# Interleaved RoPE on one core: row 0 loaded whole in fp32 and cast by ScalarE

## The chip, the cores and the metric

The kernel runs on one core of one Trainium2 chip. The metric is device microseconds (us) of one execution; of several timed runs the median is taken. Lower is better.

## What is computed

`x` has the shape (8, 2048, 16, 64) in fp32: 8 batch entries of 2048 positions, 16 heads of 64 elements. Each neighbouring pair of elements is rotated by an angle that depends on the position:

```python
x1, x2 = x[..., 0::2], x[..., 1::2]      # pairs
out1 = x1 * cos - x2 * sin               # cos, sin: (2048, 32), broadcast over batch and heads
out2 = x1 * sin + x2 * cos
out  = interleave(out1, out2)            # same shape as x, fp32
```

In and out are 67.1 MB each, so some 134 MB of fp32 have to cross between HBM and the on-chip memory (SBUF).

## The kernel before

**Tiling.** A "row" here is one batch entry. Its 2048 positions are spread over the 128 partitions, 16 positions to each (K = 16), so a row holds 16 x 1024 = 16384 elements in each partition: 64 KB in fp32, 32 KB in bf16. There are 8 rows, 0 to 7.

**Buffers.** `rows_sb` has five slots (NX = 5) of one row each in bf16. `slot(b)` sends rows 0, 1, 2 to slots 2, 3, 4 and rows 3 to 7 to slots 0 to 4. So rows 5, 6 and 7 reuse the slots of rows 0, 1 and 2, and slots 0 and 1 are empty until rows 3 and 4 are loaded into them. The buffer with the tag "work" is shared by `head` (four positions of row 0 in fp32), by `qt` (the scratch product of a rotation) and by `tail`.

**Loads and stores.** `load` and `store` issue DMAs from the POOL queue. A load casts fp32 to bf16 on the way in, and a store casts bf16 to fp32 on the way out. One DMA may move two or three rows. The exceptions are the first 4 of the 16 positions of row 0 (HEAD = 4), which come in fp32 over the SP queue into `head` and are cast by ScalarE (ACT), and the last 4 positions of row 7 (TAIL = 4), which are cast to fp32 by ScalarE and leave over the SP queue.

**Rotation.** `rotate(b, k0, k1)` is three VectorE (DVE) operations on positions k0 to k1 of a row: the product with the signed sine table into `qt` (line 83), the product with the cosine table in place (line 84), and the sum of the row with the pair-swapped `qt` (line 91). The two tables are built in bf16 from the loaded `sin` and `cos` by three small DVE operations (lines 104 to 106).

**Order.** The order is written out by hand (`manual_schedule`), and every engine and every queue works its own list from front to back. On POOL: the rest of row 0 (line 58), `cos`, `sin` (lines 97 and 98), rows 1+2 and rows 3+4 (line 60), then the stores of rows 0+1 (line 67) and 2 (line 65), the loads of row 5 and of rows 6+7 into the slots that these stores free, and the stores of rows 3 to 5, 6 and 7. On DVE: tables, row 0 in two parts (4 and 12 positions), row 1, row 2 in two halves, rows 3 to 7. A one-element copy `mark` on ScalarE, in the middle of the first half of row 2, and another one on row 0 (lines 114 and 115) hold the store of rows 0+1 back until DVE is that far. Near the end a one-element copy on ScalarE into row 6's slot (line 133) holds the last cast back until the store of row 6 has left.

Of the kernel before, what the change touches and what calls it, by code (L numbers as in the profile page):

```python
# [2 lines left out]

# [4 lines left out]


@with_exitstack  # L10
def kernel(
    ctx: ExitStack,
    tc: tile.TileContext,
    x: bass.AP,
    cos: bass.AP,
    sin: bass.AP,
    out: bass.AP,
):
    nc = tc.nc
    fp32 = mybir.dt.float32  # L20
    bf16 = mybir.dt.bfloat16
    mult = mybir.AluOpType.mult
    add = mybir.AluOpType.add

    B, S, H, D = x.shape
    P = 128
    K = S // P
    D2 = D // 2
    HD = H * D
    NX = 5  # L30
    HEAD = 4
    TAIL = 4
    HALF = 8

    x_t = x.rearrange("b (p k) h d -> p b k (h d)", p=P, k=K)
    out_t = out.rearrange("b (p k) h d -> p b k (h d)", p=P, k=K)
    cos_t = cos.rearrange("(p k) c -> p (k c)", p=P, k=K)
    sin_t = sin.rearrange("(p k) c -> p (k c)", p=P, k=K)

    consts = ctx.enter_context(tc.tile_pool(name="consts", bufs=1))  # L40
    stage = ctx.enter_context(tc.tile_pool(name="stage", bufs=1))

    cos_sb = consts.tile([P, K * D2], fp32)
    sin_sb = consts.tile([P, K * D2], fp32)
    c_tab = consts.tile([P, K, D], bf16)
    s_tab = consts.tile([P, K, D], bf16)
    mark = consts.tile([1, 1], bf16)


    def slot(b):  # L50
        return b - 3 if b >= 3 else b + 2

    rows_sb = consts.tile([P, NX, K, HD], bf16)

    def load(b, n=1, k0=0):
        s = slot(b)
        if n == 1:
            nc.gpsimd.dma_start(out=rows_sb[:, s, k0:], in_=x_t[:, b, k0:])  # L58
        else:
            nc.gpsimd.dma_start(out=rows_sb[:, s : s + n], in_=x_t[:, b : b + n])  # L60

    def store(b, n=1, k1=K):
        s = slot(b)
        if n == 1:
            nc.gpsimd.dma_start(out=out_t[:, b, :k1], in_=rows_sb[:, s, :k1])  # L65
        else:
            nc.gpsimd.dma_start(out=out_t[:, b : b + n], in_=rows_sb[:, s : s + n])  # L67

    def rotate(b, k0=0, k1=K, between=None):

        nk = k1 - k0
        xp = rows_sb[:, slot(b), k0:k1]
        qt = stage.tile([P, K, HD], bf16, name="qt", tag="work")

        def rows(a):
            return a.rearrange("p k (h e) -> p k h e", h=H, e=D)

        def tab(a):
            return dataclasses.replace(
                a, offset=a.offset + k0 * D, ap=[a.ap[0], [D, nk], [0, H], [1, D]]  # L80
            )

        nc.vector.tensor_tensor(out=rows(qt[:, :nk]), in0=rows(xp), in1=tab(s_tab), op=mult)  # L83
        nc.vector.tensor_tensor(out=rows(xp), in0=rows(xp), in1=tab(c_tab), op=mult)  # L84
        if between is not None:
            between()
        q_swap = dataclasses.replace(
            qt, offset=qt.offset + 1, ap=[qt.ap[0], [2, nk * HD // 2], [-1, 2]]
        )
        x3 = xp.rearrange("p k (a j) -> p (k a) j", j=2)  # L90
        nc.vector.tensor_tensor(out=x3, in0=x3, in1=q_swap, op=add)  # L91

    with tc.manual_schedule():
        head = stage.tile([P, HEAD, HD], fp32, name="st", tag="work")
        nc.sync.dma_start(out=head, in_=x_t[:, 0, :HEAD])
        load(0, k0=HEAD)
        nc.gpsimd.dma_start(out=cos_sb, in_=cos_t)  # L97
        nc.gpsimd.dma_start(out=sin_sb, in_=sin_t)  # L98
        load(1, 2)
        load(3, 2)  # L100

        nc.scalar.copy(out=rows_sb[:, slot(0), :HEAD], in_=head)  # L102
        s2 = s_tab.rearrange("p k (i j) -> p (k i) j", j=2)
        nc.vector.tensor_copy(out=s2[:, :, 0], in_=sin_sb)  # L104
        nc.vector.tensor_scalar_mul(s2[:, :, 1], sin_sb, -1.0)  # L105
        nc.vector.tensor_copy(  # L106
            out=c_tab.rearrange("p k (i j) -> p (k i) j", j=2),
            in_=cos_sb.to_broadcast([P, K * D2, 2]),
        )
        rotate(0, 0, HEAD)  # L110
        rotate(0, HEAD, K)
        rotate(1)

        rotate(2, 0, HALF, lambda: nc.scalar.copy(out=mark, in_=rows_sb[:1, slot(2), 0, :1]))  # L114
        nc.scalar.copy(out=rows_sb[:1, slot(0), 0, :1], in_=rows_sb[:1, slot(0), 0, :1])  # L115
        store(0, 2)
        rotate(2, HALF, K)
        store(2)
        load(5)
        load(6, 2)  # L120
        rotate(3)
        rotate(4)
        rotate(5)
        store(3, 3)
        rotate(6)
        store(6)
        rotate(7)
        store(7, k1=K - TAIL)


        tail = stage.tile([P, TAIL, HD], fp32, name="st", tag="work")
        last = rows_sb[:, slot(7)]
        nc.scalar.copy(out=rows_sb[:1, slot(6), 0, :1], in_=last[:1, K - 1, :1])  # L133
        nc.scalar.copy(out=tail, in_=last[:, K - TAIL :])  # L134
        nc.sync.dma_start(out=out_t[:, B - 1, K - TAIL :], in_=tail)


# [1 line left out]
_INS = ['x', 'cos', 'sin']  # L139
_OUTS = [((8, 2048, 16, 64), 'float32')]  # L140


# [23 lines left out]
```

## Time and profile before

| what | value |
|---|---|
| median of 3 runs | 316.18 us (316.08 to 316.18) |
| the profiled execution, its time | 316.1 us |
| the profiled execution, its span in the trace | 314.3 us |
| VectorE busy | 210.8 us, 67% of the span |
| ScalarE busy | 8.9 us, 3% |
| HBM read and written | 67.63 MB and 67.11 MB, 429 GB/s over the span |
| queue q0 (POOL), share of the 16 DMA engines | 96.8% |
| queue q1 (SP), share of the 16 DMA engines | 3.3% |

The span is what the trace covers; the profiled execution's time is 1.8 us longer. A DMA is worked by 16 DMA engines that each serve 8 of the 128 partitions. The GB/s of a stretch count the bytes as they are on the SBUF side of a load and on the HBM side of a store. A load that casts fp32 to bf16 therefore shows half of what it reads, and a store shows what it writes.

### The profile page before, as it was taken

To read this page: it belongs to the slowest core of one execution; us is meant where nothing else is said; L and a number is where in the kernel's file an instruction comes from. 1 tells how busy PE (TensorE), PEld (TensorE's weight loads), DVE (VectorE), ACT (ScalarE), POOL (GpSimd) and SP (SyncE) were. 2 spreads that over 40 slices of the span, in tenths; PEclk is the share of its full clock that TensorE was granted. 3 is DMA by queue.
4 is the path that set the end of the run, shared out by engine and by line. 5 is a ranking of instruction groups with operands and counts; after the bars stand their busy time and mean duration, and the time that the engine had idled before them with its cause. 6 is when DMAs were issued, how large, how long until landed. Compare 5 with 4: busy or idle time off the path is not lost.

```text
span 314.3 us, 116 instructions
## 1 busy us (share of the span) xinstructions
DVE 210.8 (67%) x33; ACT 8.9 (3%) x6; POOL 7.8 (2%) x16
## 2 busy tenths in 40 slices
DVE  0009995099999999999993399903999999200000
ACT  1040000000000000000000000000000000000400
POOL 4000000000000000000000000000000000000000
DMA  8999999999999999999999999999999999999997
GB/s 256 261 284 200 200 204 263 200 200 217 250 200 267 442 492 400 400 475 459 400 200 246 221 200 200 250 217 334 400 509 425 400 400 525 409 400 400 434 434 334
DMA packets 2656, 102.24 MB, mean 325 GB/s; under 512 B 224, under 2 KB 224, under 8 KB 352
## 3 DMA queue, kind: packets, MB, share of 16 engines
q0 software_dynamic: 2368, 98.04, 96.8%
q1 hardware_dynamic: 288, 4.19, 3.3%
HBM read 67.63 MB, written 67.11 MB: 429 GB/s over the span
## 4 chain that ended last, share of the span: by engine, by line
another core or an unknown queue 66%; DVE 20%; ACTq 1%; ACT 0%; issue 0%; DVEq 0%
DVE rows_sb L84 7%; DVE qt L83 7%; DVE rows_sb L91 6%; ACTq L161 1%; DVE c_tab L106 0%; ACT rows_sb L133 0%; ACT mark L114 0%; ACT rows_sb L115 0%; ACTq L133 0%; DVEq L83 0%
## 5 line engine op out<-in xcount | busy, mean ns | idle before, releaser
L83 DVE TENSOR_TENSOR qt<-rows_sb,s_tab 128x16384 bf16<-128x16384 bf16 (+3 forms) x10 | 69.8, 6984 | 33.7 <-DMA rows_sb<-in_x_dram 33.5
L91 DVE TENSOR_TENSOR rows_sb<-rows_sb,qt 128x16384 bf16<-128x16384 bf16 (+3 forms) x10 | 69.8, 6985 | 0.6 <-ACT mark L114 0.3
L84 DVE TENSOR_TENSOR rows_sb<-rows_sb,c_tab 128x16384 bf16<-128x16384 bf16 (+3 forms) x10 | 69.8, 6984 | 0.3
L104 DVE CAST s_tab<-sin_sb 128x512 bf16<-128x512 f32 x1 | 0.5, 454 | 23.8 <-DMA sin_sb<-in_sin_dram 23.8
L133 ACT COPY rows_sb<-rows_sb 1x1 bf16<-1x1 bf16 x1 | 0.2, 193 | 196.5 <-DMA out_dram<-rows_sb 196.5
L67 POOL DMA_DIRECT2D out_dram<-rows_sb x2 | 1.5, 740 | 138.5 <-ACT rows_sb L115 93.7
L102 ACT CAST rows_sb<-st 128x4096 bf16<-128x4096 f32 x1 | 3.6, 3604 | 13.2 <-DMA st<-in_x_dram 13.2
L65 POOL DMA_DIRECT2D out_dram<-rows_sb x3 | 1.7, 567 | 80.4 <-DVE rows_sb L91 80.4
L134 ACT CAST st<-rows_sb 128x4096 f32<-128x4096 bf16 x1 | 3.6, 3598 | 0.0
L60 POOL DMA_DIRECT2D rows_sb<-in_x_dram x3 | 2.2, 740 | 18.8 <-DMA out_dram<-rows_sb 18.8
L114 ACT COPY mark<-rows_sb 1x1 bf16<-1x1 bf16 x1 | 0.2, 193 | 78.7 <-DVE rows_sb L84 78.7
L58 POOL DMA_DIRECT2D rows_sb<-in_x_dram x2 | 1.2, 609 | 24.3 <-DMA out_dram<-rows_sb 23.5
L102 ACT ACT_TABLE_LOAD x1 | 1.3, 1283 | 0.7 <-PEq L150 0.7
L106 DVE CAST c_tab<-cos_sb 128x1024 bf16<-128x1024 f32 x1 | 0.7, 685 | 0.0
L98 POOL DMA_DIRECT2D sin_sb<-in_sin_dram x1 | 0.6, 564 | 0.0
L97 POOL DMA_DIRECT2D cos_sb<-in_cos_dram x1 | 0.6, 557 | 0.0
L105 DVE TENSOR_SCALAR s_tab<-sin_sb 128x512 bf16<-128x512 f32 x1 | 0.4, 444 | 0.0
L115 ACT COPY rows_sb<-rows_sb 1x1 bf16<-1x1 bf16 x1 | 0.2, 189 | 0.0
L150 POOL MEMSET const-float32-0.0<- 128x1 f32 x1 | 0.1, 99 | 0.2 <-issue 0.2
L150 POOL MEMSET const-bfloat16-1.0<- 128x1 bf16 x1 | 0.1, 102 | 0.0
L150 POOL MEMSET const-float32-1.0<- 128x1 f32 x1 | 0.1, 99 | 0.0
L150 POOL MEMSET const-uint8-127<- 128x1 uint8 x1 | 0.1, 99 | 0.0
## 6 DMA issues: line engine op xcount, KB each, us to landing
rows_sb<-in_x_dram POOLq DMA_DIRECT2D x3, 8192.0 KB, 59.4
out_dram<-rows_sb POOLq DMA_DIRECT2D x1, 6144.0 KB, 40.9
rows_sb<-in_x_dram POOLq DMA_DIRECT2D x1, 4096.0 KB, 38.3
rows_sb<-in_x_dram POOLq DMA_DIRECT2D x1, 3072.0 KB, 21.2
st<-in_x_dram SPq DMA_DIRECT2D x1, 2048.0 KB, 14.5
out_dram<-st SPq DMA_DIRECT2D x1, 2048.0 KB, 15.5
cos_sb<-in_cos_dram POOLq DMA_DIRECT2D x1, 256.0 KB, 21.2
sin_sb<-in_sin_dram POOLq DMA_DIRECT2D x1, 256.0 KB, 21.3
```

The lines of the kernel that those rows point to most:

```text
L58: nc.gpsimd.dma_start(out=rows_sb[:, s, k0:], in_=x_t[:, b, k0:])
L60: nc.gpsimd.dma_start(out=rows_sb[:, s : s + n], in_=x_t[:, b : b + n])
L65: nc.gpsimd.dma_start(out=out_t[:, b, :k1], in_=rows_sb[:, s, :k1])
L67: nc.gpsimd.dma_start(out=out_t[:, b : b + n], in_=rows_sb[:, s : s + n])
L83: nc.vector.tensor_tensor(out=rows(qt[:, :nk]), in0=rows(xp), in1=tab(s_tab), op=mult)
L84: nc.vector.tensor_tensor(out=rows(xp), in0=rows(xp), in1=tab(c_tab), op=mult)
L91: nc.vector.tensor_tensor(out=x3, in0=x3, in1=q_swap, op=add)
L97: nc.gpsimd.dma_start(out=cos_sb, in_=cos_t)
L102: nc.scalar.copy(out=rows_sb[:, slot(0), :HEAD], in_=head)
L106: nc.vector.tensor_copy(out=c_tab.rearrange("p k (i j) -> p (k i) j", j=2), in_=cos_sb.to_broadcast([P, K * D2, 2]),)
L134: nc.scalar.copy(out=tail, in_=last[:, K - TAIL :])
L161: with _tile.TileContext(nc) as tc:
```

## The change

Row 0 no longer comes in two pieces. One DMA of the SP queue brings all of it in fp32 into `wide`, a view of slots 0 and 1 (2 x 32 KB in each partition, 64 KB in fp32). ScalarE casts it in four parts of four positions each into slot 2. The load of rows 3+4, which goes to slots 0 and 1, is written behind these casts. VectorE rotates row 0 in four parts of four positions, where it took two parts before. The POOL queue's first load (the 12 positions of row 0) and the buffer `head` are gone.

```diff
-    HEAD = 4
+    PART = 4
...
+    wide = rows_sb[:, :2].rearrange("p s k e -> p (s k e)").bitcast(fp32)
+    wide = wide.rearrange("p (k e) -> p k e", k=K)
+
-    def load(b, n=1, k0=0):
+    def load(b, n=1):
         s = slot(b)
         if n == 1:
-            nc.gpsimd.dma_start(out=rows_sb[:, s, k0:], in_=x_t[:, b, k0:])
+            nc.gpsimd.dma_start(out=rows_sb[:, s], in_=x_t[:, b])
...
-        head = stage.tile([P, HEAD, HD], fp32, name="st", tag="work")
-        nc.sync.dma_start(out=head, in_=x_t[:, 0, :HEAD])
-        load(0, k0=HEAD)
+
+        nc.sync.dma_start(out=wide, in_=x_t[:, 0])
         nc.gpsimd.dma_start(out=cos_sb, in_=cos_t)
         nc.gpsimd.dma_start(out=sin_sb, in_=sin_t)
         load(1, 2)
+
+        for k in range(0, K, PART):
+            nc.scalar.copy(out=rows_sb[:, slot(0), k : k + PART], in_=wide[:, k : k + PART])
         load(3, 2)
-
-        nc.scalar.copy(out=rows_sb[:, slot(0), :HEAD], in_=head)
         s2 = s_tab.rearrange("p k (i j) -> p (k i) j", j=2)
...
-        rotate(0, 0, HEAD)
-        rotate(0, HEAD, K)
+        for k in range(0, K, PART):
+            rotate(0, k, k + PART)
         rotate(1)
```

## The prediction

> **What bounds the kernel now.** I read the page's head and its DMA rows first, then the windows around the start, the first store and the end, and then the timeline of VectorE and POOL up to that store.
>
> ```profile
> DMA  8999999999999999999999999999999999999997
> ...
> q0 software_dynamic: 2368, 98.04, 96.8%
> q1 hardware_dynamic: 288, 4.19, 3.3%
> HBM read 67.63 MB, written 67.11 MB: 429 GB/s over the span
> ```
>
> The DMA engines are full in every slice but the first and the last, while VectorE works 67% of the span. The windows show how little is left:
>
> ```profile
> 0.00:2.00 2.00, 0.00 (x0) 1.26 (x1) 0.96 (x6) 1.00 0.45 98
> 62.00:98.00 36.00, 35.15 (x6) 0.29 (x2) 0.00 (x0) 1.00 1.00 215
> 98.00:100.00 2.00, 2.00 (x1) 0.00 (x0) 0.71 (x1) 1.00 0.46 98
> 100.00:102.00 2.00, 2.00 (x1) 0.00 (x0) 0.00 (x0) 1.00 1.23 524
> 312.00:314.30 2.30, 0.00 (x0) 0.00 (x0) 0.00 (x0) 1.00 0.27 114
> ```
>
> The last two columns are the DMA share and GB/s. Packets are counted where they start, so short windows swing (0.46, then 1.23: one round falls into the next window); a long one shows the pace, 215 GB/s of bf16, which is 430 of fp32 read. The first packet starts at 2.0 us and the last ends near 313.4 (packet records of the trace), so 134.74 MB take 311.4 us: 433 GB/s, 27.0 for each of 16 engines. A row of 8.39 MB is 19.4 us; one partition's 64 KB, of which every engine has 8 in a row, is 2.42 us. So 311 of 314.3 us are bytes at this pace. A change that moves the same bytes can only pay by the rest, or cost by opening a hole. A hole opens where a transfer is issued too late. The places near the change:
>
> ```profile
> 15.27 3.60 ACT L102 CAST rows_sb<-st 128x4096 bf16<-128x4096 f32 x1 [13.25 <-DMA st<-in_x_dram]
> 23.80 0.45 DVE L104 CAST s_tab<-sin_sb 128x512 bf16<-128x512 f32 x1 [23.80 <-DMA sin_sb<-in_sin_dram]
> ...
> 25.08 2.29 DVE L83 TENSOR_TENSOR qt<-rows_sb,s_tab 128x4096 bf16<-128x4096 bf16 x1
> 27.40 2.29 DVE L84 TENSOR_TENSOR rows_sb<-rows_sb,c_tab 128x4096 bf16<-128x4096 bf16 x1
> 29.73 2.29 DVE L91 TENSOR_TENSOR rows_sb<-rows_sb,qt 128x4096 bf16<-128x4096 bf16 x1
> ...
> 62.46 8.69 DVE L83 TENSOR_TENSOR qt<-rows_sb,s_tab 128x16384 bf16<-128x16384 bf16 x1 [10.67 <-DMA rows_sb<-in_x_dram]
> ...
> 98.14 0.71 POOL L67 DMA_DIRECT2D out_dram<-rows_sb  x1 [93.69 <-ACT rows_sb L115]
> ```
>
> VectorE is done with row 0 at 51.8 and waits 10.67 us for rows 1+2, which land at 62.4. From there runs the one tight chain: row 1 (26.2 us), half of row 2 and the two marks, the store of rows 0+1 at 98.14. Its first packets start at 100.4, right behind the last load: a lead of 2.3 us, part of which the issue itself needs. Whatever delays VectorE's start on row 1 eats this lead and then leaves the engines idle.
>
> **The change part by part.**
>
> *Bytes.* Row 0 is 8.39 MB of fp32 read whichever queue brings it. Both queues go at one pace: between 3 and 5 us the SP queue alone moves 426 to 475 GB/s; the casting loads read 430. A casting load writes half as much into SBUF, and the trace shows no gain in pace from that. The sum until rows 1+2 are in is the same 25.7 MB (row 0, tables 0.52, two rows): 59.4 us from 2.0 on, and the landing stays near 62.4. 0 us.
>
> *Start.* SP issues at 0.74 us as before. The POOL queue, first issued at 1.24, has its first packets at 5.6; until then SP's queue feeds the engines alone, before with 8 packets of 16 KB for each engine (4.9 us of work), now with 8 of 64 KB (19.4 us). Covered in both, 0 us. The first round of packets is slower than the later ones (mean 1.12 us where 0.61 follows): half a microsecond of latency. As a fixed latency it stays; as a factor on the packet it would grow (third rival).
>
> *Row 0's landing.* Head and POOL queue took turns packet by packet: 5 of 8 head packets were through at 5.6, the other 3 each waited for a turn of 48 KB read (2.42 us for the pair), which gives 12.9, one more turn before the completion 14.7, and it landed at 15.24. Now each turn of SP is 2.42 us, and what POOL's queue has first is small: the tables, 8 packets of 4 KB an engine at 0.16 us and two completions. With 2 of SP's 8 packets through at 5.6 us the other 6 alternate with 6 of these. Row 0 is through after 2.4 + 8 x 2.42 + 6 x 0.16 = 22.7 us and, with skew and completion as above, lands at about 23.5; the tables land at about 24 (23.8 before). Rows 1+2 then have the engines to themselves.
>
> The Trainium skill (DMA: Bandwidth & Descriptors, Queues, rings and completion order) says that an engine drains a whole packet, typically 9 to 17 descriptors, from one ring before it turns to the next. By that all of row 0 would pass in one turn and land about 1 us earlier. The trace differs: the head, 8 such pieces an engine, would then have landed near 7 us, and it landed at 15.24.
>
> *Casts.* Four of 3.60 us (line 102, the same shape) in place of one: 23.5 to 37.9. Behind them on ScalarE stand only the marks, due at 97.5.
>
> *Rotation of row 0.* Four parts of 25.08 to 32.05 = 6.97 us, 27.9 in place of 26.7. The first waits for the first cast, at 27.1; the later ones find theirs done (3.6 beside 7.0 us). VectorE is done at 55.1 in place of 51.8. Cover: it would wait for 62.4 anyway, so 7.3 us are left of the 10.67. 0 us.
>
> *The load of rows 3+4.* Its issue moves from 3.7 to 37.9, since POOL stands in its queue until the last cast. Queued behind it on POOL is the store of rows 0+1, due at 98. The engines need this load at 62.4, when rows 1+2 run out. Cover 24.5 us; even with the longest time seen from an issue to first packets (1.24 to 5.6, 4.4 us) 20 us remain. 0 us. If the cover were gone, each us of lateness would cost one us.
>
> *After 62.4.* Waits, order and sizes are those of before. One DMA less on POOL saves its completion, 0.02 us of each engine.
>
> Sum: 0 us on 316.1 of the profiled execution; the median of the runs shown is 0.08 above it. I forecast 316.15.
>
> **The rivals.**
>
> *SP's row 0 is cut into small packets and starves (slower).* No transfer of q1 with over 16 KB in a partition is in the trace: 288 packets are 256 of 16 KB and 32 completions. If the queue cuts at 16 KB, row 0 has 32 packets an engine, 5 of them gone at 5.6 us. Ten go with the tables until 13, and the rest alternate one for one with 16 packets of 2.42 us of rows 1+2, the last of which are through only near 62. Then row 0 lands at 62: casts to 76.5; load of rows 3+4 issued there; VectorE's parts 65.7 to 93.6, row 1 to 119.8, the rest of the chain (9.5 us) to 129.3. The store comes 31.2 us late, less the lead 2.3: +28.9, 345 us. It decides where row 0 lands after about 31 us (62.4 less 27.9 and the first cast); cut at 32 KB (16 packets) it lands at 30 to 32, which costs 0 to 1. Against: every large packet seen is one partition's whole run: 16 KB on q1, 64 KB in q0's stores (2048 data packets carry 97.5 MB). 0.06.
>
> The Trainium skill (DMA: Bandwidth & Descriptors, SWDGE vs HWDGE vs iDMA) puts a packet of the software queue at preferably 4096 bytes or less. If the SP queue held to that, row 0 would starve as in this rival; the trace's tables do so (128 packets of 4 KB for 512 KB), its rows do not.
>
> *Parts don't overlap (the change doesn't do what it says).* If VectorE's first part waited for all four casts, it would run 37.9 to 65.8, 3.4 us past 62.4, less the lead: +1.1, 317.2. Against: in the order of the compiled instructions each part has its own wait on ScalarE. 0.02.
>
> *The slow first round is a factor.* 1.12 against 0.61 on a 2.42 us packet is 2.0 us lost where 0.5 is lost now: +1.5, 317.6. For it: nothing but the bound. 0.05.
>
> *Faster.* Idle are the first 2.0 us, 0.2 around 3 us and the end; the change touches only the 0.2. Beyond 0.63 us I see no source but one the trace doesn't show. 315.3, 0.04.
>
> **How the numbers follow.** 0.2% is 0.63 us, about what a measurement of this kernel can tell from no change. The forecast, in which all of it stays covered, has 0.83 and by itself spans 315.8 to 316.5 (the runs' 0.1 us, the start's 0.2, another 0.2 in landings). Reaching to the small slower costs (lead partly used up, a 32 KB cut, part of the first-round bound) the range is 315.7 to 317.1. The starving case is left out at the top. Faster 0.04, same 0.83, slower 0.13.
>
> **What would show it.** Right: casts start near 23.5 and end near 38; POOL's issue of rows 3+4 near 38; VectorE still waits some 7 us for a DMA at 62.4; the store of rows 0+1 at 98.1; no slice of the DMA row under 9 but the ends. Wrong: casts that start after 31 us, a first row-1 product later than 62.5, or a hole in the DMA row between 62 and 105.

## The result, and the profile after

The changed kernel takes 316.80 us, median of 22 runs (316.56 to 317.42), against 316.15 for the kernel before. The ratio is 1.0015 (95% interval 1.0009 to 1.0021): slower by some 0.5 us by the ratio and by 0.65 us by the medians, which is small, but clear of no change. The time lies inside the range, and the ratio inside the 0.2% that I called "same", though its interval just reaches past it; the forecast of no change at all was wrong.

The page of the changed kernel, with the same rows as before: its slices, its queues, its HBM bytes.

```profile
DMA  9999999999999999999999999999999999999997
...
q0 software_dynamic: 2224, 94.90, 92.1%
q1 hardware_dynamic: 288, 10.49, 8.0%
HBM read 67.63 MB, written 67.11 MB: 428 GB/s over the span
```

Row 0 has moved from q0 to q1. q1 still has 288 packets, with 6.3 MB more in them: in the packet records 128 packets of 64 KB bring row 0, where 128 of 16 KB brought its head, so SP's queue did not cut it. HBM bytes are the same and the DMA row has no hole. The windows (the last two columns are the DMA share and GB/s):

```profile
0.00:2.00 2.00, 0.00 (x0) 1.27 (x1) 0.94 (x6) 1.00 1.29 426
62.00:98.00 36.00, 35.03 (x6) 0.29 (x2) 0.00 (x0) 1.00 0.98 211
98.00:100.00 2.00, 2.00 (x1) 0.00 (x0) 0.70 (x1) 1.00 0.92 197
100.00:102.00 2.00, 2.00 (x1) 0.00 (x0) 0.00 (x0) 1.00 1.23 524
312.00:314.50 2.50, 0.00 (x0) 0.00 (x0) 0.00 (x0) 1.00 0.26 111
```

The load of rows 3+4 hands over to the store of rows 0+1 between 98 and 102 as it did before; that the first window has 426 means only that the first packets are larger and are counted whole where they start. The timeline of the steps that the prediction named:

```profile
23.56 14.13 ACT L104 CAST rows_sb<-rows_sb 128x4096 bf16<-128x4096 f32 x4 [21.55 <-DMA rows_sb<-in_x_dram]
23.88 0.46 DVE L107 CAST s_tab<-sin_sb 128x512 bf16<-128x512 f32 x1 [23.88 <-DMA sin_sb<-in_sin_dram]
...
27.20 2.29 DVE L86 TENSOR_TENSOR qt<-rows_sb,s_tab 128x4096 bf16<-128x4096 bf16 x1 [1.96 <-ACT rows_sb L104]
...
37.98 0.73 POOL L63 DMA_DIRECT2D rows_sb<-in_x_dram  x1 [34.78 <-ACT rows_sb L104]
...
62.58 8.69 DVE L86 TENSOR_TENSOR qt<-rows_sb,s_tab 128x16384 bf16<-128x16384 bf16 x1 [7.30 <-DMA rows_sb<-in_x_dram]
...
98.26 0.70 POOL L70 DMA_DIRECT2D out_dram<-rows_sb  x1 [59.55 <-ACT rows_sb L118]
```

Row 0 lands at 23.56, the casts end at 37.7, POOL issues at 37.98, VectorE waits another 7.30 us for rows 1+2, and everything from there on is 0.12 us later than before. Inside the kernel the picture is the predicted one, but for one sign: the first product of row 1, at 62.58, is past the 62.5 that the prediction set as a mark of being wrong. The kernel before with a later load of rows 3+4 (the first of the two below) has 62.58 too and takes the time of before, so that mark was set inside the scatter.

Where, then, is the difference? Each run has a time and a span, and most of the difference lies outside what the trace covers:

| | time, us | span, us | time outside the span, us |
|---|---|---|---|
| before, profiled execution | 316.1 | 314.3 | 1.8 |
| after, profiled execution | 316.64 | 314.5 | 2.1 |
| before, median of 33 runs beside the first experiments | 316.17 | 314.4 | 1.77 (1.73 to 1.83) |
| after, median of 22 runs | 316.80 | 314.65 | 2.15 (2.12 to 2.20) |

The larger part, 0.38 us, is outside the span, and the two ranges do not touch. Some 0.2 us are inside it.

### The profile page after: what moved, and what is told of

The parts are those of the page before. It is cut to its first block, busy times and chain, and to the rows that moved or that the text cites. A ratio compares the mean times of both kernels' runs of the same rounds, so it can differ in the third digit from the quotient of the medians.

```text
span 314.5 us, 126 instructions
## 1 busy us (share of the span) xinstructions
DVE 211.9 (67%) x39; ACT 19.4 (6%) x9; POOL 7.3 (2%) x15
## 4 chain that ended last, share of the span: by engine, by line
another core or an unknown queue 51%; DMA 20%; DVE 20%; ACT 1%; ACTq 1%; issue 0%; DVEq 0%
DMA out_dram<-rows_sb 13%; DMA rows_sb<-in_x_dram 7%; DVE rows_sb L87 7%; DVE qt L86 7%; DVE rows_sb L94 6%; ACT rows_sb L104 1%; ACTq L164 1%; ACT rows_sb L136 0%; ACT mark L117 0%; ACT rows_sb L118 0%; DVEq L86 0%; ACTq L136 0%
## 5 line engine op out<-in xcount | busy, mean ns | idle before, releaser
L86 DVE TENSOR_TENSOR qt<-rows_sb,s_tab 128x16384 bf16<-128x16384 bf16 (+2 forms) x12 | 70.2, 5847 | 32.6 <-DMA rows_sb<-in_x_dram 30.2
L94 DVE TENSOR_TENSOR rows_sb<-rows_sb,qt 128x16384 bf16<-128x16384 bf16 (+2 forms) x12 | 70.2, 5847 | 0.6 <-ACT mark L117 0.3
L87 DVE TENSOR_TENSOR rows_sb<-rows_sb,c_tab 128x16384 bf16<-128x16384 bf16 (+2 forms) x12 | 70.2, 5847 | 0.4
L104 ACT CAST rows_sb<-rows_sb 128x4096 bf16<-128x4096 f32 x4 | 14.1, 3602 | 21.5 <-DMA rows_sb<-in_x_dram 21.5
L63 POOL DMA_DIRECT2D rows_sb<-in_x_dram x3 | 2.2, 722 | 53.5 <-ACT rows_sb L104 34.8
L61 POOL DMA_DIRECT2D rows_sb<-in_x_dram x1 | 0.5, 546 | 23.5 <-DMA out_dram<-rows_sb 23.5
```

The lines of the kernel that those rows point to most:

```text
L104: nc.scalar.copy(out=rows_sb[:, slot(0), k : k + PART], in_=wide[:, k : k + PART])
```

## The experiments

Below, "outside" is the median over a kernel's runs of time less span. "Records" are all of VectorE's entries in the trace, its waits and synchronisation included: 47 before, 55 after (six products and two semaphore waits more). Every kernel stands beside runs of the kernel before on the same chip.

### The time outside the span: VectorE's list

**Six more products alone** (kernel before, row 0 in four parts):

```diff
-        rotate(0, HEAD, K)
+        for k in range(HEAD, K, HEAD):
+            rotate(0, k, k + HEAD)
```

> Kernel before with one edit: VectorE rotates the 12 positions of row 0 in three parts of four, so that it issues the 6 more products of the change and nothing else moves. Instruction theory (the change's 0.35 us outside the span comes from VectorE's longer list): time outside the span 2.1 us where before has 1.8, span 314.3, in all +0.3 to +0.4 us. Rival (the cost comes with row 0's new path over SP): outside 1.8, +0.0.

Measured: 316.16 beside 316.17, outside 1.76, 53 records. The instruction theory failed as stated.

**The six products taken out of the changed kernel:**

```diff
-        for k in range(0, K, PART):
-            rotate(0, k, k + PART)
+        rotate(0, 0, PART)
+        rotate(0, PART, K)
```

> Changed kernel with VectorE's two parts of row 0 (4 and 12 positions) as before: 6 products fewer than the changed kernel, the transfer and the four casts kept. VectorE then waits for the last cast at 37.7 and is done at 57.5, before rows 1+2 land at 62.5. Instruction theory: outside 1.8, in all 0.3 to 0.4 us below the changed kernel, so +0.1 to +0.2 against before. Rival: outside stays 2.1, time that of the changed kernel, +0.5 to +0.6.

Measured: 316.36, outside 1.77, span 314.6, 47 records. Here the instruction theory held: the 0.38 us are gone, though SP's load, the casts and the late load are all in place. So it does hang on VectorE's list, and yet six more instructions do not bring it by themselves. Either it needs ScalarE's three more casts too (a limit on the whole program), or VectorE's list has a limit between 53 and 55 records.

**Nine more products** (kernel before), and **14 ScalarE copies** (kernel before):

```diff
-        rotate(0, HEAD, K)
+        for k in range(HEAD, K, 3):
+            rotate(0, k, k + 3)
```

> Kernel before with the 12 positions of row 0 in four parts of three: 9 more products on VectorE (56 records of it in the trace, 55 in the changed kernel, 53 in the run with 6 more), nothing on ScalarE. If VectorE's own list passes a limit between 53 and 55 records: outside 2.15, +0.4 us. If the limit lies in the whole program or needs ScalarE's three more casts: outside 1.77, +0.0.

```diff
         nc.scalar.copy(out=rows_sb[:, slot(0), :HEAD], in_=head)
+        for _ in range(14):
+            nc.scalar.copy(out=mark, in_=head[:1, 0, :1])
```

> Kernel before with 14 one-element ScalarE copies behind the head's cast, at a time when ScalarE idles: 130 records in the whole trace or more, where the changed kernel has 126, VectorE's list as before. If the limit is one on the whole program: outside 2.15, +0.4 us. If it is VectorE's own: outside 1.77, +0.0.

Measured: with nine more products 316.56 (ratio 1.0010, 1.0002 to 1.0019), outside 2.19, span 314.4 as before; with the copies 316.14, outside 1.77, at 130 records in the whole trace. It is VectorE's list, not the program's length.

**Three products fewer** (kernel before, `rotate(0)` in one part):

> Kernel before with row 0 rotated in one part: 3 products fewer on VectorE, done with row 0 at 51.5 as before. If the time outside the span goes by steps, this either stays on the step of before (1.77, 0.0) or reaches a lower one (1.4, -0.4 us, a version faster than both); if it went by the instruction, 0.06 us for each (0.38 over 6): outside 1.6, -0.2.

Measured: 316.15, outside 1.76, 44 records. No lower step, and nothing by the instruction.

I then took it for a limit: 54 or 55 records and more cost 0.4 us. The changed kernel with four SP loads (below) spoilt this: 57 records, outside 1.81. Three kernels told a limit from a window:

```diff
+        nc.vector.tensor_copy(out=mark, in_=sin_sb[:1, :1])
         rotate(0, 0, HEAD)
-        rotate(0, HEAD, K)
+        for k in range(HEAD, K, 3):
+            rotate(0, k, k + 3)
```

> Kernel before with row 0 in five parts and one more one-element VectorE copy: 57 VectorE records (56 gave 2.19 us outside the span; the changed kernel with four SP loads has 57 and gave 1.81). Window theory (VectorE's list costs 0.4 us where its end falls in a narrow range of lengths): outside 1.8. Limit theory (every list from 54 or 55 on costs it, and the four SP loads took it away in some other way): outside 2.15.

The same copy in front of four parts of four:

> Kernel before with row 0 in four parts and one more one-element VectorE copy: 54 VectorE records, between 53 (1.76) and 55 (2.15). It places the lower edge; both theories allow either value: 1.77 or 2.15, nothing in between.

And seven parts (4 and six of 2), without it:

> Kernel before with the 12 positions of row 0 in six parts of two: 15 more products, some 62 VectorE records. VectorE is done with row 0 near 53, covered. Window theory: outside 1.8. Limit theory: outside 2.15 or more.

Measured: outside 1.75 with 57 records, 2.04 with 54, and 1.81 with 62. One VectorE instruction more than the five parts makes the kernel faster: 316.24 where those have 316.56 (in another set, whose kernel before has 316.17 where this one's has 316.13). At 54 records neither theory's "nothing in between" holds: 2.04 (2.02 to 2.08) is lower than 2.15.

If that is so, the changed kernel must get faster by instructions that do nothing for it. One-element copies behind its tables (line 113 on), first two, then three of them:

```diff
+        for _ in range(3):
+            nc.vector.tensor_copy(out=mark, in_=sin_sb[:1, :1])
         for k in range(0, K, PART):
             rotate(0, k, k + PART)
```

> Changed kernel with two one-element VectorE copies added behind the tables: 57 VectorE records, past the window of 54 to 56. Window theory: outside 1.77, so 0.38 us faster than the changed kernel for more instructions. The rest of the loss, if it is the first round of 64 KB packets, stays: span 0.2 above before, 316.35 in all.

> Changed kernel with three one-element VectorE copies behind the tables (two gave 56 VectorE records, still in the window): 57 records. Window theory: outside 1.77, 0.38 us below the changed kernel. First-round theory: span 0.2 above before, as in the other runs with 64 KB packets, 316.35 in all.

Two copies made 56 records, not the 57 that I had counted on, and stayed inside the window: 316.97, outside 2.17. Three made 57: 316.40, outside 1.75 (1.72 to 1.81), where the changed kernel beside the first of these two has 316.72 and 2.16:

> The changed kernel itself beside these two, on one chip: 316.7 to 316.8, outside 2.15, span 0.2 above before. All theories give the same here; it is the base for the two others.

All that was measured of it, by length of VectorE's list:

| records | kernel | outside, us |
|---|---|---|
| 44 | before, row 0 in one part | 1.76 |
| 47 | before; changed with two parts; before with 14 ScalarE copies | 1.77; 1.77; 1.77 |
| 47 | before with rows 3+4 held back, less and more (below) | 1.80; 1.81 |
| 48 | changed, SP in two loads and two parts; before, head in two loads (both below) | 1.77; 1.75 |
| 53 | before, four parts | 1.76 |
| 54 | before, four parts, one copy | 2.04 |
| 55 | changed | 2.15 and 2.16 |
| 56 | before, five parts; changed, two copies; changed, SP in two loads | 2.19; 2.17; 2.17 |
| 57 | before, five parts, one copy; changed, three copies; changed, SP in two loads, one copy | 1.75; 1.75; 1.77 |
| 57 | changed, SP in four loads | 1.81 |
| 62 | before, seven parts | 1.81 |

The window is shown, on both kernels. What happens in it is not. The Trainium skill (Runtime: NRT & Kernel Launch, Instruction fetch mechanics) says that an engine's instructions are fetched in blocks ahead of their use and that crossing a block's end costs little, mostly hidden. A block's end that falls among the last instructions of VectorE, where no work hides its fetch, would give such a window. This is a guess, and the kept traces do not bear it out. Their packet records hold a queue for instructions, q14: in every kernel its packets of 8 KB start 7.3 to 10.6 us ahead of the span. A single one lies behind a span, 1.2 us after the end of the kernel with seven parts (62 records), which does not have the 0.4 us. Behind the spans of the kernels with 54, 55 and 56 records there is none, as far as the trace reaches. What else shifts with the length of the list is open.

### The 0.2 us inside the span: the first packets

**SP's load in two pieces** (changed kernel), so that the first 8 packets of each engine are of 16 KB again:

```diff
-        nc.sync.dma_start(out=wide, in_=x_t[:, 0])
+        nc.sync.dma_start(out=wide[:, :PART], in_=x_t[:, 0, :PART])
+        nc.sync.dma_start(out=wide[:, PART:], in_=x_t[:, 0, PART:])
```

> Changed kernel with SP's load of row 0 cut into 4 and 12 positions, so that the first round of packets is of 16 KB again. First-round theory (the 0.14 us more inside the span is the first round, which loses more on a 64 KB packet): span 0.1 to 0.2 us below the changed kernel, first product of row 1 at 62.4 to 62.5. Rival (the difference inside the span is run-to-run scatter): span as in the changed kernel, 314.5 to 314.7. Either way outside stays 2.1.

Measured: 316.63, span 314.4 (314.6 with the load in one piece and two parts, in the same set), outside 2.17. First product of row 1 at 62.51, against 62.58, which tells nothing: in other kept traces it comes at 62.54 with 64 KB first packets (the changed kernel measured again) and at 62.87 with 16 KB (two loads and one VectorE copy, below).

**The same, with VectorE's two parts,** and **the same with one VectorE copy** (57 records):

> Changed kernel with both suspects undone: SP's load in 4 and 12 positions, and VectorE's row 0 in two parts; whole row 0 over SP, the four casts and the late load of rows 3+4 stay. If the two terms are independent and complete: outside 1.77, span 314.4, 316.17 as before (0.0). If something in the new path costs by itself (rival), 316.3 or more stays.

> As the padded changed kernel (57 VectorE records by one copy), but SP's load of row 0 in 4 and 12 positions. Both terms theory: outside 1.77 and span as before, 316.2, 0.15 to 0.2 us below the padded kernel with SP's load in one piece. Rival (the 0.2 inside the span has another cause in the new path): 316.35, as that kernel.

Measured: 316.27 with span 314.5 and outside 1.77 (ratio 1.0002, 0.9993 to 1.0011), and 316.31 with span 314.55 and outside 1.77. With both terms taken care of, the changed kernel cannot be told from the one before, though it keeps the whole row over SP, the casts and the late load.

Over all sets, the mean spans are 314.46 us for the kernel before (145 runs, standard error 0.02), 314.70 for the five kernels with 64 KB first packets (64 runs, 0.03), and 314.56 for the three with 16 KB first packets (34 runs, 0.04). Of 0.24 us the first packets account for 0.14 (standard error 0.05); the other 0.10 (0.04) stay open. The packet records agree in size. The first packet of an engine takes 1.12 us on average before, where 0.61 follows, and 3.15 after, where 2.42 follows: a loss of 0.51 and of 0.73 in these two executions. Over all kept traces the loss is 0.55 us with 16 KB first packets (14 traces, 0.43 to 0.63) and 0.70 with 64 KB (5 traces, 0.59 to 0.74). So most of it does not grow with the packet, and some 0.15 us does.

**Smaller first packets yet** (kernel before, the head's load in 1 and 3 positions):

```diff
-        nc.sync.dma_start(out=head, in_=x_t[:, 0, :HEAD])
+        nc.sync.dma_start(out=head[:, :1], in_=x_t[:, 0, :1])
+        nc.sync.dma_start(out=head[:, 1:], in_=x_t[:, 0, 1:HEAD])
```

> Kernel before with the head's load over SP in 1 and 3 positions, so that the first round of packets is of 4 KB where it was of 16 KB. If the first round's loss grows with its packet (0.2 us more in the span at 64 KB than at 16 KB): span 0.05 to 0.15 us below before, a version faster than both. If a part of it is a fixed latency that 16 KB already shows whole: span 314.4 as before, 0.0.

Measured: 316.75 (ratio 1.0013, 1.0004 to 1.0022), span 315.0. Neither expectation held: this cut of the head loses half a microsecond more. It is not the first 4 KB packets that lose it. Four rounds of them are slow (0.47, 0.33, 0.22 and 0.17 us, where 0.16 follows), which makes 0.55 us, as much as one round of 16 KB. By the bytes moved, the kernel is 0.04 to 0.13 us behind seven kernels with 16 KB first packets at 4 us, and 0.44 to 0.54 behind them at 8 us. The loss falls on the start of the second load, whose first four packets take 0.53 to 0.58 us where later ones of the same 12 KB take 0.47; why they do is open, and so is whether small first packets would pay without a second load close behind.

### The terms that the prediction had at nothing

**The late load.** In the kernel before, rows 3+4 are held back until VectorE is done with row 0, and then until it has both products of row 1:

```diff
         load(1, 2)
-        load(3, 2)
...
         rotate(0, HEAD, K)
+        nc.scalar.copy(out=rows_sb[:1, slot(3), 0, :1], in_=rows_sb[:1, slot(0), K - 1, :1])
+        load(3, 2)
```

> Kernel before with the load of rows 3+4 held back by a one-element ScalarE copy until VectorE is done with row 0, so POOL issues it near 52 us, 14 us later than the changed kernel does. Cover theory: the engines need it only at 62.4, the span stays 314.3, +0.0 (at most +0.1 for one more ScalarE instruction). Rival (a late issue already costs something at the hand-over at 62.4, which would make it the changed kernel's loss): a hole in the packets near 62.4 and +0.3 us or more.

```diff
         load(1, 2)
-        load(3, 2)
...
-        rotate(1)
+        rotate(1, between=lambda: nc.scalar.copy(out=rows_sb[:1, slot(3), 0, :1], in_=rows_sb[:1, slot(1), K - 1, :1]))
+        load(3, 2)
```

> Kernel before with the load of rows 3+4 held back until VectorE has made both products of row 1, so POOL issues it near 80.2, 18 us after rows 1+2 ran out. Cover theory: each us past 62.1 less the time from issue to first packets costs one; hole of 19 to 22.5 us in the packets, +19 to +22.5 us in all (335 to 339). If VectorE or the stores later take some of it back: less than +15.

The first was issued at 52.45 us, 14 later than in the changed kernel, and took 316.17, as before:

```profile
52.45 0.73 POOL L60 DMA_DIRECT2D rows_sb<-in_x_dram  x1 [48.72 <-ACT rows_sb L111]
62.58 8.69 DVE L83 TENSOR_TENSOR qt<-rows_sb,s_tab 128x16384 bf16<-128x16384 bf16 x1 [10.65 <-DMA rows_sb<-in_x_dram]
```

The second was issued at 80.36 and took 338.40 (two runs): +22.2. Its windows:

```profile
60.00:62.00 2.00, 0.00 (x0) 0.00 (x0) 0.00 (x0) 1.00 0.01 0
62.00:64.00 2.00, 1.58 (x1) 0.00 (x0) 0.00 (x0) 1.00 0.00 0
64.00:80.00 16.00, 15.81 (x2) 0.13 (x1) 0.00 (x0) 1.00 0.00 0
80.00:82.00 2.00, 1.90 (x1) 0.07 (x1) 0.73 (x1) 1.00 0.91 147
```

The engines stand still from 62 to past 81, some 20 us, and nothing later gives them back. The other 2 us are in packets of the late load itself: the first of each engine takes 3.13 us where 2.43 is usual (0.7 us), and later ones, most of all the last at 119 us (3.46 us), add 1.4. So a hole costs at least what it lasts, and the changed kernel's issue at 37.98 is far from one.

**Turns on the queues.** Row 0 over SP in four loads of four positions (changed kernel), 32 packets of 16 KB an engine in place of 8 of 64:

```diff
-        nc.sync.dma_start(out=wide, in_=x_t[:, 0])
+        for k in range(0, K, PART):
+            nc.sync.dma_start(out=wide[:, k : k + PART], in_=x_t[:, 0, k : k + PART])
```

> Changed kernel with row 0 over SP in four loads of four positions, so that it comes in 32 packets of 16 KB an engine in place of 8 of 64 KB; each part's cast waits for its own load. Turn theory (one packet a turn, so small packets starve behind rows 1+2): the third part lands near 37, the fourth only near 61.5; POOL issues rows 3+4 at 65.3, a hole in the packets from 62 on, VectorE done with row 0 at 72, store of rows 0+1 issued near 108, +7 to +11 us (324 to 328). If SP's queue gets a share by bytes or goes first: all parts are there by 45, +0.0 against the changed kernel.

Measured: 325.76 us (two runs, ratio 1.0294, 1.0273 to 1.0315), with outside 1.81. The timeline, casts and the load behind them:

```profile
8.54 3.60 ACT L105 CAST rows_sb<-rows_sb 128x4096 bf16<-128x4096 f32 x1 [6.52 <-DMA rows_sb<-in_x_dram]
...
21.21 3.60 ACT L105 CAST rows_sb<-rows_sb 128x4096 bf16<-128x4096 f32 x1 [9.06 <-DMA rows_sb<-in_x_dram]
...
47.91 3.60 ACT L105 CAST rows_sb<-rows_sb 128x4096 bf16<-128x4096 f32 x1 [23.10 <-DMA rows_sb<-in_x_dram]
...
62.58 3.60 ACT L105 CAST rows_sb<-rows_sb 128x4096 bf16<-128x4096 f32 x1 [11.07 <-DMA rows_sb<-in_x_dram]
...
66.48 0.73 POOL L63 DMA_DIRECT2D rows_sb<-in_x_dram  x1 [63.27 <-ACT rows_sb L105]
...
108.87 0.70 POOL L70 DMA_DIRECT2D out_dram<-rows_sb  x1 [41.67 <-ACT rows_sb L119]
```

Behind the tables every packet of SP pays for one of rows 1+2, and the fourth part lands only when those are through, at 62.58 (61.5 expected; the third came later than I had it, 47.91 for 37). The load of rows 3+4 is then late, and after it the store at 108.87. The same bytes in smaller packets are 9 us slower, so packets take turns whatever their size. The prediction's starving rival is a real mechanism; SP's queue does not bring it about by itself, since it leaves a 64 KB run whole.

## Why the prediction was right and wrong

**Right, step by step.** Bytes and pace: same HBM bytes, no hole. Landing of row 0: 23.5 predicted, 23.56 measured, by the turns that the four loads then showed. One reading in it was loose: at 5.6 us only one of SP's eight 64 KB packets was through, not two, and POOL's first packet started at 7.1; as POOL's turns are then 0.16 us each, the sum hardly moves. Tables 24 and 23.88. Casts to 37.9 and 37.7; issue of rows 3+4 37.9 and 37.98. VectorE's remaining wait before row 1: 7.3 and 7.30. Store of rows 0+1: 98.1 and 98.26. The cover of the late load was real, as the two late loads show from both sides of its edge. The Trainium skill's rule (DMA: Bandwidth & Descriptors, Queues, rings and completion order) that an engine drains a whole packet of typically 9 to 17 descriptors before the next ring has its turn would, by the prediction's estimate, have put row 0 a microsecond earlier; it did not land earlier.

**Wrong: "After 62.4" and the sum.** The prediction made its sum "on 316.1 of the profiled execution" and treated the 1.8 us between span and time as a constant that no edit touches. It is not one: the row 0 loop in four parts lengthened VectorE's list to 55 records, and there this piece is 2.15 us. That is the failed step: of the six products and the two waits that come with them only duration and cover were costed, at 0 us, and not that instructions are also a list. This is 0.38 of the 0.65 us between the medians. That the length does it is shown; by what mechanism is open. No view of the profile of before shows it; what the prediction could have had is the line "span to time, 1.8, not known to stay" with a bound.

**Mis-sized: the start.** "As a fixed latency it stays; as a factor on the packet it would grow." The truth is between them and nearer to the latency: 0.14 us go with the first packets' size, where the two ends were 0 and 1.5. The forecast took 0. It is the second, smaller term, and together with the 0.10 that stay open it makes the span's 0.24.

**Luck: the range.** By itself, the forecast with all costs covered spanned 315.8 to 316.5, and 316.80 is outside that. The time is inside the wider range because room was left there for a used-up lead, a 32 KB cut and part of the first-round bound. Of these only the last happened, with 0.14 us; the larger term had no place in the range.

**The rivals.** Starving: did not happen, its mechanism is real. Parts that do not overlap: no, VectorE's first part started at 27.20, ten microseconds before the last cast's end. The first round as a factor: a tenth of it. Faster: no.

## What to carry to other kernels

In this kernel, where DMA is full from end to end, moving a load from one queue to another changed the order and hardly the time. The question was whether each transfer is issued before the engines run dry: an issue 14 us later than that of the changed kernel was free, and one beyond the cover left a hole of 20 us and cost 22.2. The two queues shared an engine by packets, not by bytes: row 0 landed at 23.56 us in 64 KB packets and at 62.58 in 16 KB packets. So a queue that must be quick beside another should have the larger packets. And below a microsecond, look at the time outside the span before looking for a cause inside. One or two VectorE instructions more moved it here by 0.4 us either way, so compare kernels only with that piece taken apart.

## What the hardware showed that I had not expected

- The time outside the span is 1.75 to 1.81 us for VectorE lists of 44 to 53 and of 57 and 62 records, and 2.04, 2.15 and 2.17 to 2.19 us for 54, 55 and 56. ScalarE's list (15 to 29 records) does not move it.
- The first packet of each engine loses 0.55 us with 16 KB and 0.70 with 64 KB (means over 14 and 5 traces); in the changed kernel 64 KB costs 0.14 us over 16 KB. Cutting the head's load into 4 and 12 KB, in the kernel before, made its span 315.0 us where 314.5 stood beside it.
- After a hole of 20 us the whole run was 22.2 us longer; the other 2 us are in slower packets of the load behind the hole (3.13 us for the first of each engine, where 2.43 is usual), and why the last ones are slow too is open.
